# Staging of paired weight blocks: six tiles owned by each phase in place of four shared ones

## The chip, the cores and the metric

The kernel runs on one core of one Trainium2 chip. The metric is the device time of one execution in microseconds; the figure compared is the median of several runs. Profiled executions are taken one at a time, and their views (engine busy shares, waits, chains of waits, timelines) come from a single execution.

## The reference

One decoder layer for 256 tokens of width 4096, all in float32. One projection feeds two mixers: gated linear attention (branch A) and sliding-window attention with sinks (branch B). Each branch is projected to 4096 columns, the two are merged by sigmoid gates, projected once more and added to x.

```
h = rms_norm(x, norm_gains)
z = h @ w_in                       # gq gk gv gg gdec | sq sk sv sg | ga gb
o_a = gla_mix(gq, gk, gv, log_a)   # chunked linear attention, 8 heads
y_a = (rms_norm(o_a) * silu(gg)) @ w_gla_out
o_b = swa_sink_mix(sq, sk, sv, sinks)
y_b = (o_b * silu(sg)) @ w_swa_out
merged = sigmoid(ga + b_gates[0]) * y_a + sigmoid(gb + b_gates[1]) * y_b
out = rms_norm(x + merged @ w_out, final_norm_gain)
```

Nearly all of the work is in products of a 256-row left side with weights that are read once from memory, some 477 MB.

## The kernel before

Every float32 product is made of three matmuls: both operands are split into a high half (a cast on ACT, L141) and a low half (a subtraction on DVE, L142), and hi·hi, hi·lo and lo·hi are summed in PSUM (L160 to L162, L232 to L234). The left sides (hT, oaT, obT, mT) stay in SBUF in both halves; weights stream through.

**Phases.** The program goes through these in order: the blocks gq, gk, gv, gg of branch A (`gemm`, L145); the projection ya of branch A (`spilled`, four pairs of column blocks, ya0 to ya3); branch B (sk, sv, sq, sg with `gemm`, and its attention); the projection yb (yb0 to yb3); eight gate pairs in the order ga0, gb0, ga1, gb1 and so on; 64 transposes that make mT; the last projection o in four pairs; the final norm. The results of ya and yb are spilled to memory and read back by the gates (tiles yga, ygb, fetched by DMAs that ACT issues).

**A pair.** `pair` (L186) multiplies the left side with two column blocks of 512 at once. Its loop runs over blocks j of the depth, 8 in ya and yb, 16 in the gates and o. Each j loads two tiles of 512 KB, r_j and s_j, on SP's queue (L206, L208). For most j there are eight products of a tile and its hi/lo halves: 24 matmuls. For the j in `SEVEN` (0, 2, 5 of 8; 0, 3, 5, 8, 10, 13 of 16) there are seven, 21 matmuls, by a scheme in Strassen's manner: DVE forms sums of the loaded tiles, t in L212 (from r and s), u in L213 and the new s in L214, and four tiles t, u, r, s are split into halves. The left sides of those products are sums too; `combine` (L165) makes them (tiles a and d on DVE, cast and subtraction into xca, xcb, xch or xcm). The first pair of ya, yb and o has eight products at every j, so that its combine can run beside it. For the gates, the combine of hT into xch is run by `then` behind the second pair of yb (L272), and all eight gate pairs have sevens. A pair of 8 with sevens has 183 matmuls, one of 16 has 366, one of 16 without sevens 384. `outputs` (L247) adds the seven sums up; its first sum is held in tile v.

**Buffers.** The loaded tiles (tag raw) come from one pool `stage` with four buffers (L72) that all phases share. Halves come from the pool of the phase `cur["hl"]`, with a ring of three for `gemm` and of five for `pair` (`cur["n"]`); so do t, u and v. The y tiles of the gates and the x tiles of o have a ring of two, tag "yr".

**Order.** The Tile scheduler sets each engine's order; loads, casts and low halves are written at raised priority (PRIO 400 in `gemm`, PRM 120 in `pair`), and each engine runs its list in order. SP issues the weight loads one after the other, and each waits for the last reader of the buffer that it gets.

Of the kernel before, what the change touches and what calls it, by code (L numbers as in the profile page):

```python
# [48 lines left out]
def trunk_kernel(  # L49
# [95 lines left out]
    def gemm(name, lhs, w, nkt, before=None, chunks=WHOLE):  # L145

        acc = [acc_ps.tile([P, NB], F32, tag="acc", name=f"{name}_a{t}") for t in range(NT)]
        for k0, n in [c for c in chunks if c[0] < nkt]:
            if before is not None:
                before(k0, n)  # L150
            with tc.high_priority(PRIO):
                raw = stage.tile([P, n, NB], F32, tag="raw", name=f"{name}_r{k0}")
# [12 lines left out]
    def combine(lhs, xc, js, name):  # L165


        for c, j in enumerate(js):
# [472 lines left out]
    for n in range(NP2):  # L641
# [101 lines left out]
```

## Time and profile before

| | us |
|---|---|
| median of 3 runs (2613.38 to 2619.92) | 2614.85 |
| the profiled execution | 2607.58 |
| its span in the trace | 2605.8 |
| TensorE busy in it | 2503.3 |
| DVE busy in it | 1759.6 |
| ACT busy in it | 1219.4 |

The span runs from the first instruction to the last in the trace. Busy time is the time in which an engine has an instruction running; matmuls are pipelined, so a busy TensorE isn't TensorE at its peak. The phases stand in the trace one behind the other: ya about 600 to 783 us, yb to 1488, the gates to 2215, o to 2591. A "pair" below is the stretch of TensorE's time from its first matmul to the next pair's first.

### The profile page before, as it was taken

The page shows a single profiled execution, that of the slowest core. Times are in us where ns is not written, and L with a number is a line of the kernel's source. Part 1 is how long each engine was busy: PE and PEld are TensorE (multiplying, and loading weights), DVE is VectorE, ACT ScalarE, POOL GpSimd, SP SyncE. Part 2 cuts the span into 40 slices and gives each one's busy share as a digit, 9 for nine tenths or more (in the row PEclk, how much of TensorE's full clock was granted, in tenths as well). Part 3 has the DMA queues.
Part 4 walks back from the last instruction along what each step waited for, and adds up shares of the span by engine and source line. Part 5 has one row for each costly group of instructions (what it writes and reads, how often), then busy time and mean ns, then how long its engine had stood idle before and what let it go on. Part 6 is the DMA issues. An engine that isn't in the chain of part 4 may idle for free.

```text
span 2605.8 us, 29359 instructions
## 1 busy us (share of the span) xinstructions
PE 2503.3 (96%) x10968; PEld 1996.1 (77%) x10968; DVE 1759.6 (68%) x1967; ACT 1219.4 (47%) x1488; POOL 41.9 (2%) x52
## 2 busy tenths in 40 slices
PE   8999999999999999999998999999999999999997
PEld 6778888887777888888786777777787777778765
DVE  7554555546774455555568778878878887857777
ACT  6444354434453344444544444445445445545444
POOL 4000000000000000000000000000000000000000
PEclk9999999999999999999998999999999999999999
DMA  7556556555666645555465666666666666555655
GB/s 254 150 172 187 166 178 185 170 169 166 222 202 202 186 151 175 159 148 184 130 201 163 205 214 203 194 217 198 200 201 207 206 199 220 184 179 193 217 190 190
DMA packets 139024, 491.14 MB, mean 188 GB/s; under 512 B 15840, under 2 KB 16224, under 8 KB 138880
## 3 DMA queue, kind: packets, MB, share of 16 engines
q1 hardware_dynamic: 127296, 461.69, 55.7%
q10 hardware_dynamic: 11584, 27.57, 3.1%
q8 instruction: 86, 1.41, 0.2%
q14 instruction: 58, 0.48, 0.1%
HBM read 476.61 MB, written 12.58 MB: 188 GB/s over the span
## 4 chain that ended last, share of the span: by engine, by line
PE 53%; DVE 24%; DMA 17%; issue 4%; ACT 1%; POOL 0%; ACTq 0%; SPq 0%; DVEq 0%; POOLq 0%
DMA ga_s<-in_wgate_dram 5%; DMA gb_s<-in_wgate_dram 4%; DMA o_s<-in_wout_dram 4%; PE sg_a L161 2%; PE gv_a L161 2%; PE sq_a L162 2%; PE sq_a L160 2%; PE gv_a L160 2%; PE sq_a L161 2%; PE gv_a L162 2%; PE sg_a L160 2%; PE sg_a L162 2%; PE gg_a L162 2%; PE gg_a L160 2%; PE gg_a L161 2%
## 5 line engine op out<-in xcount | busy, mean ns | idle before, releaser
L212 DVE TENSOR_TENSOR gb_t<-gb_r,gb_s 128x1024 f32<-128x1024 f32 x24 | 29.4, 1224 | 28.8 <-DMA gb_s<-in_wgate_dram 28.8
L212 DVE TENSOR_TENSOR ga_t<-ga_r,ga_s 128x1024 f32<-128x1024 f32 x24 | 29.4, 1224 | 24.0 <-DMA ga_s<-in_wgate_dram 24.0
L212 DVE TENSOR_TENSOR o_t<-o_r,o_s 128x1024 f32<-128x1024 f32 x18 | 22.0, 1225 | 32.4 <-DMA o_s<-in_wout_dram 32.3
L101 POOL TENSOR_TENSOR sf<-sf,mhalf 128x1 f32<-128x1 f32 x2 | 1.1, 550 | 1824.5 <-DVE sf L100 1824.5
L119 DVE SCALAR_TENSOR_TENSOR hT<-xsb,gin_sb,hT 128x256 fp32r<-128x256 f32 x32 | 26.1, 865 | 5.3 <-ACT hT L118 5.3
L565 ACT ACTIVATE s<-s,mx 128x128 f32<-128x128 f32 x64 | 28.4, 445 | 0.0
L128 POOL TENSOR_TENSOR ssq<-ssq,sq 128x512 f32<-128x512 f32 x15 | 25.6, 1709 | 24.5 <-ACT sq L127 23.9
L627 ACT ACTIVATE gb_d<-gb_d 128x512 f32<-128x512 f32 x16 | 10.1, 632 | 24.0 <-DVE gb_d L626 23.9
L212 DVE TENSOR_TENSOR ya_t<-ya_r,ya_s 128x1024 f32<-128x1024 f32 x9 | 11.0, 1225 | 14.5 <-DMA ya_s<-in_wgla_dram 14.4
L550 DVE SCALAR_TENSOR_TENSOR s<-s,mask 128x384 f32<-128x384 f32 x32 | 16.0, 552 | 6.0 <-PE s L549 6.0
L212 DVE TENSOR_TENSOR yb_t<-yb_r,yb_s 128x1024 f32<-128x1024 f32 x9 | 11.0, 1223 | 11.5 <-DMA yb_s<-in_wswa_dram 11.5
L656 ACT ACTIVATE xt<-x 128x512 f32<-128x512 f32 x16 | 10.0, 627 | 15.9 <-DVE x L245 15.9
L141 ACT CAST sg_16h<-sg_r 128x1024 fp32r<-128x1024 f32 x4 | 4.2, 1050 | 28.1 <-PE sg_a L162 28.1
L214 DVE TENSOR_TENSOR gb_s<-gb_u,gb_s 128x512 f32<-128x512 f32 x24 | 16.6, 690 | 0.5
L213 DVE TENSOR_TENSOR ga_u<-ga_t,ga_r 128x512 f32<-128x512 f32 x24 | 16.6, 690 | 0.5
L214 DVE TENSOR_TENSOR ga_s<-ga_u,ga_s 128x512 f32<-128x512 f32 x24 | 16.6, 690 | 0.5
L213 DVE TENSOR_TENSOR gb_u<-gb_t,gb_r 128x512 f32<-128x512 f32 x24 | 16.5, 688 | 0.4
L473 DVE COPY oraw<-op 128x512 f32<-128x512 f32 x8 | 5.5, 692 | 15.6 <-PE op L472 15.6
L118 ACT ACTIVATE hT<-xsb,gin_sb 128x256 fp32r<-128x256 f32 x32 | 14.0, 498 | 2.6 <-DMA xsb<-in_xT_dram 2.2
L582 DVE COPY pT<-pt 128x384 f32<-128x384 f32 x16 | 8.9, 555 | 9.3 <-PE pt L579 9.3
L141 ACT CAST gb_t10h<-gb_t 128x1024 fp32r<-128x1024 f32 x4 | 4.2, 1053 | 23.1 <-DVE gb_t L212 17.8
L579 PE MATMUL pt<-ident,s 128*128 128x128 f32 x96 | 15.0, 279 | 0.0
(2815 smaller groups left out, 9027.0 us busy)
## 6 DMA issues: line engine op xcount, KB each, us to landing
gv_r<-in_win_dram SPq DMA_DIRECT2D x64, 512.0 KB, 4.0
gg_r<-in_win_dram SPq DMA_DIRECT2D x64, 512.0 KB, 3.9
sq_r<-in_win_dram SPq DMA_DIRECT2D x64, 512.0 KB, 3.6
sg_r<-in_win_dram SPq DMA_DIRECT2D x64, 512.0 KB, 3.6
ga_r<-in_wgate_dram SPq DMA_DIRECT2D x64, 512.0 KB, 4.8
ga_s<-in_wgate_dram SPq DMA_DIRECT2D x64, 512.0 KB, 5.8
gb_r<-in_wgate_dram SPq DMA_DIRECT2D x64, 512.0 KB, 5.2
gb_s<-in_wgate_dram SPq DMA_DIRECT2D x64, 512.0 KB, 5.6
```

The source lines that it names most:

```text
L118: nc.scalar.activation(hT[:, kt, 0, :], xsb[:, kt, :], AF.Copy, scale=g)
L119: nc.vector.scalar_tensor_tensor(hT[:, kt, 1, :], xsb[:, kt, :], g, hT[:, kt, 0, :].bitcast(F32), ALU.mult, ALU.subtract)
L128: nc.gpsimd.tensor_tensor(ssq, ssq, sq, ALU.add)
L160: nc.tensor.matmul(acc[t], lh, hi[:, i, :], start=kt == 0, stop=False)
L161: nc.tensor.matmul(acc[t], lh, lo[:, i, :], start=False, stop=False)
L162: nc.tensor.matmul(acc[t], ll, hi[:, i, :], start=False, stop=kt == nkt - 1)
L212: nc.vector.tensor_tensor(ts, r1, r2[:, 0:1, :].broadcast_to([P, 2, NB]), ALU.add)
L213: nc.vector.tensor_tensor(t2[:, 0, :], ts[:, 1, :], r1[:, 0, :], ALU.add)
L214: nc.vector.tensor_tensor(r2[:, 0, :], t2[:, 0, :], r2[:, 1, :], ALU.add)
L550: nc.vector.scalar_tensor_tensor(s4[:, jj * 2 + half, :], sps[:, 0 : 3 * P], HD**-0.5, mask2, ALU.mult, ALU.add)
L565: nc.scalar.activation(s4[:, k, cs], s4[:, k, cs], AF.Exp, bias=mx[:, k, t : t + 1], accum_out=sm[:, k, t : t + 1],)
L579: nc.tensor.transpose(tp[:, m * P : (m + 1) * P], s4[:, k, m * P : (m + 1) * P], ident)
```

## The change

The staging tiles `raw` no longer come from a pool that all phases share, but from the pool of the phase, with `cur["r"]` buffers: four where `gemm` runs and six where `pair` runs (ya; yb, gates and o). v of `outputs` moves into the ring "yr" of two, which the gates' y tiles and o's x tiles use; d of `combine` shares the buffer of t; xcb and xch share one buffer, and st and sf one with "ev". Because xch can now be written only when yb is done with xcb, the combine of hT moves from behind yb1 to behind ga0's products, and ga0 has eight products at every j, 384 matmuls in place of 366.

```diff
-    stage = ctx.enter_context(tc.tile_pool(name="stage", bufs=4))
...
-                raw = stage.tile([P, n, NB], F32, tag="raw", name=f"{name}_r{k0}")
+                raw = cur["hl"].tile([P, n, NB], F32, tag="raw", name=f"{name}_r{k0}", bufs=cur["r"])
...
-            d = cur["hl"].tile([P, 4, P], F32, tag="v", name=f"{name}d{j}")
+            d = cur["hl"].tile([P, 4, P], F32, tag="t13", name=f"{name}d{j}")
...
-                r1 = stage.tile([P, 2, NB], F32, tag="raw", name=f"{name}_r{j}")
+                r1 = cur["hl"].tile([P, 2, NB], F32, tag="raw", name=f"{name}_r{j}", bufs=cur["r"])
                 nc.sync.dma_start(r1, w[j][:, 0:2, :])
-                r2 = stage.tile([P, 2, NB], F32, tag="raw", name=f"{name}_s{j}")
+                r2 = cur["hl"].tile([P, 2, NB], F32, tag="raw", name=f"{name}_s{j}", bufs=cur["r"])
...
-    def outputs(q, d, name):
+    def outputs(q, d, name, pool):
 
         if 1 in q:
-            v = cur["hl"].tile([P, NB], F32, tag="v", name=f"{name}_v")
+            v = pool.tile([P, NB], F32, tag="yr", name=f"{name}_v", bufs=2)
...
-            if n == 1 and then is not None:
-                then()
...
     with phase("hl0") as cur["hl"], phase("gla") as gp:
-        cur["n"] = STG
+        cur["n"], cur["r"] = STG, 4
...
     with phase("hl1") as cur["hl"], phase("yap") as yp:
-        cur["n"] = STM
+        cur["n"], cur["r"] = STM, 6
...
     with phase("hl2") as cur["hl"], phase("swa") as sp:
-        cur["n"] = STG
+        cur["n"], cur["r"] = STG, 4
...
-    cur["hl"], cur["n"] = ctx.enter_context(phase("hl3")), STM
-    cur["n"] = STM
+    cur["hl"] = ctx.enter_context(phase("hl3"))
+    cur["n"], cur["r"] = STM, 6
     xp = ctx.enter_context(phase("xp"))
+    ep = ctx.enter_context(phase("ep"))
+    xcb = xp.tile([P, len(SEVEN[OKT // 2]), 4, 2, P], F32R, tag="xc", name="xcb")
+    spilled("yb", obT, wswa, yb_d, xcb, ep)
     xch = xp.tile([P, len(SEVEN[KT // 2]), 4, 2, P], F32R, tag="xc", name="xch")
-    with phase("ybp") as yp:
-        xcb = yp.tile([P, len(SEVEN[OKT // 2]), 4, 2, P], F32R, name="xcb")
-        spilled("yb", obT, wswa, yb_d, xcb, yp, lambda: combine(hT, xch, SEVEN[KT // 2], "h"))
-    ep = ctx.enter_context(phase("ep"))
...
-            q = pair(f"{kind}{n}", hT, wgate[w * NP2 + n], KT // 2, xc=xch)
+            q = pair(f"{kind}{n}", hT, wgate[w * NP2 + n], KT // 2, xc=None if n + w == 0 else xch)
+            if n + w == 0:
+                combine(hT, xch, SEVEN[KT // 2], "h")
...
-    st = ep.tile([P, NT, NBLK], F32, name="st")
+    st = ep.tile([P, NT, NBLK + 1], F32, tag="ev", name="st")
```

The order of SP's loads is the same in both kernels. What moves stands on DVE and ACT, at three places. Rows are one engine's list, each line an instruction with the tile that it writes and those that it reads; line numbers of the changed kernel are lower by one to three.

DVE at the passage from yb1 to yb2, before, in two pieces: the first sums of yb2, then the combine of hT (ha, hd, xch), which begins here,

```order
L212 TENSOR_TENSOR yb2_t0_10023<-yb2_r0_10019,yb2_s0_10021 128x1024
L245 TENSOR_TENSOR yb_d1_9944<-yb1_q5_9619,yb_d1_9944 128x512
L175 TENSOR_TENSOR hd0_9959<-ha0_9957 128x128
L176 TENSOR_TENSOR hd0_9959<-ha0_9957 128x128
L177 TENSOR_TENSOR hd0_9959<-hd0_9959,ha0_9957 128x128
L142 TENSOR_TENSOR yb2_t0l_10029<-yb2_t0_10023,yb2_t0h_10028 128x1024
L178 TENSOR_TENSOR hd0_9959<-ha0_9957,hd0_9959 128x128
L170 TENSOR_TENSOR ha3_9966<-hT_87 128x512
L180 TENSOR_TENSOR xch_9287<-hd0_9959,xch_9287 128x4x128
```

and some thirty rows further its end, with what follows of yb2:

```order
L178 TENSOR_TENSOR hd13_10004<-ha13_10002,hd13_10004 128x128
L213 TENSOR_TENSOR yb2_u0_10024<-yb2_t0_10023,yb2_r0_10019 128x512
L180 TENSOR_TENSOR xch_9287<-hd13_10004,xch_9287 128x4x128
L214 TENSOR_TENSOR yb2_s0_10021<-yb2_u0_10024,yb2_s0_10021 128x512
L142 TENSOR_TENSOR yb2_u0l_10033<-yb2_u0_10024,yb2_u0h_10032 128x512
L142 TENSOR_TENSOR yb2_r0l_10037<-yb2_r0_10019,yb2_r0h_10036 128x1024
L142 TENSOR_TENSOR yb2_s0l_10041<-yb2_s0_10021,yb2_s0h_10040 128x1024
```

The same place now:

```order
L211 TENSOR_TENSOR yb2_t0_9965<-yb2_r0_9961,yb2_s0_9963 128x1024
L141 TENSOR_TENSOR yb1_s7l_9913<-yb1_s7_9906,yb1_s7h_9912 128x1024
L212 TENSOR_TENSOR yb2_u0_9966<-yb2_t0_9965,yb2_r0_9961 128x512
L141 TENSOR_TENSOR yb2_t0l_9971<-yb2_t0_9965,yb2_t0h_9970 128x1024
L213 TENSOR_TENSOR yb2_s0_9963<-yb2_u0_9966,yb2_s0_9963 128x512
L141 TENSOR_TENSOR yb2_u0l_9975<-yb2_u0_9966,yb2_u0h_9974 128x512
L244 TENSOR_TENSOR yb1_v_9941<-yb1_q6_9616,yb_d1_9940 128x512
L211 TENSOR_TENSOR yb2_t2_10047<-yb2_r2_10043,yb2_s2_10045 128x1024
L141 TENSOR_TENSOR yb2_r0l_9979<-yb2_r0_9961,yb2_r0h_9978 128x1024
```

All rows of ha, hd and xch are gone from between yb2's t0 and u0; they stand from behind yb3's fifth block into ga0.

ACT at the start of ya (oaT is its left side, made from transposes oa3_t0 and oa3_t2), before:

```order
L278 CAST oaT_803<-oa3_t0_4224 128x2x256
L141 CAST ya0_r0h_4255<-ya0_r0_4251 128x1024
L141 CAST ya0_s0h_4259<-ya0_s0_4253 128x1024
L141 CAST ya0_r1h_4291<-ya0_r1_4287 128x1024
L141 CAST ya0_s1h_4295<-ya0_s1_4289 128x1024
L278 CAST oaT_803<-oa3_t2_4231 128x2x256
```

and now:

```order
L275 CAST oaT_800<-oa3_t0_4221 128x2x256
L275 CAST oaT_800<-oa3_t2_4228 128x2x256
L613 DMA bt00_10633<-in_bgates_dram 128x1024
L178 CAST xca_4243<-yad0_4545 128x4x128
L140 CAST ya0_r0h_4252<-ya0_r0_4248 128x1024
L140 CAST ya0_s0h_4256<-ya0_s0_4250 128x1024
```

The second cast of oaT, a load of the gates' bias and the first cast of xca have moved ahead of the first half ya0_r0h.

DVE in ga2, where the gate of gb1 is finished, from the use of its second y tile (ygb101) to that of its fourth, before:

```order
L245 TENSOR_TENSOR gb_d1_13375<-gb_d1_13375,ygb101_13392 128x512
L626 SCALAR_TENSOR_TENSOR gb_d1_13375<-gb_d1_13375,rstd_81,bt11_12729 128x512
L245 TENSOR_TENSOR m_10693<-m_10693,gb_d1_13375 128x512
L142 TENSOR_TENSOR ga2_r4l_13589<-ga2_r4_13584,ga2_r4h_13588 128x1024
L142 TENSOR_TENSOR ga2_s4l_13593<-ga2_s4_13586,ga2_s4h_13592 128x1024
L245 TENSOR_TENSOR gb_d1_13375<-gb_d1_13375,ygb110_13398 128x512
L626 SCALAR_TENSOR_TENSOR gb_d1_13375<-gb_d1_13375,rstd_81,bt11_12729 128x512
L245 TENSOR_TENSOR m_10693<-m_10693,gb_d1_13375 128x512
L212 TENSOR_TENSOR ga2_t5_13624<-ga2_r5_13620,ga2_s5_13622 128x1024
L245 TENSOR_TENSOR gb_d1_13375<-gb_d1_13375,ygb111_13404 128x512
```

and now:

```order
L244 TENSOR_TENSOR gb_d1_13298<-gb_d1_13298,ygb101_13315 128x512
L624 SCALAR_TENSOR_TENSOR gb_d1_13298<-gb_d1_13298,rstd_78,bt11_12652 128x512
L244 TENSOR_TENSOR m_10632<-m_10632,gb_d1_13298 128x512
L141 TENSOR_TENSOR ga2_r4l_13512<-ga2_r4_13507,ga2_r4h_13511 128x1024
L624 SCALAR_TENSOR_TENSOR gb_d1_13298<-gb_d1_13298,rstd_78,bt11_12652 128x512
L141 TENSOR_TENSOR ga2_s4l_13516<-ga2_s4_13509,ga2_s4h_13515 128x1024
L244 TENSOR_TENSOR gb_d1_13298<-gb_d1_13298,ygb110_13321 128x512
L211 TENSOR_TENSOR ga2_t5_13547<-ga2_r5_13543,ga2_s5_13545 128x1024
L244 TENSOR_TENSOR m_10632<-m_10632,gb_d1_13298 128x512
L244 TENSOR_TENSOR gb_d1_13298<-gb_d1_13298,ygb111_13327 128x512
```

Between the two uses stand eight rows in both lists; what is new is that the buffer of ygb111 is that of ygb101, and that one step of the gate and the addition to m have changed places with s4l and t5.

## Rows read from the trace of the kernel before

**Rows 1.** The page, part 1: busy time, share of the span and instructions

```profile
PE 2503.3 (96%) x10968; PEld 1996.1 (77%) x10968; DVE 1759.6 (68%) x1967; ACT 1219.4 (47%) x1488; POOL 41.9 (2%) x52
```

**Rows 2.** Stretches: length, busy time of each engine, granted clock, DMA share, GB/s

```profile
649.10:691.50 42.40, 42.40 (x185) 34.44 (x184) 33.53 (x35) 22.13 (x25) 0.00 (x0) 1.00 0.64 211
691.50:783.00 91.50, 87.06 (x368) 70.05 (x367) 68.79 (x75) 42.63 (x45) 1.34 (x4) 0.98 0.62 207
1341.40:1383.80 42.40, 42.40 (x184) 34.45 (x183) 33.08 (x38) 20.15 (x23) 0.00 (x0) 1.00 0.67 211
1383.80:1442.00 58.20, 45.26 (x185) 35.36 (x183) 47.29 (x70) 24.43 (x29) 0.00 (x0) 0.88 0.49 163
1442.00:1488.30 46.30, 43.25 (x185) 34.08 (x184) 36.63 (x40) 22.17 (x25) 0.00 (x0) 1.00 0.62 205
1488.30:1577.30 89.00, 86.29 (x367) 68.36 (x366) 67.31 (x70) 41.30 (x46) 0.00 (x0) 1.00 0.65 213
1577.30:2215.20 637.90, 612.27 (x2579) 483.10 (x2577) 518.82 (x564) 315.49 (x348) 0.00 (x0) 0.99 0.62 204
2316.00:2591.40 275.40, 261.56 (x1099) 205.76 (x1097) 212.63 (x232) 132.34 (x162) 0.55 (x1) 0.99 0.59 192
```

**Rows 3.** Waits of TensorE: total, times, longest

```profile
PE yb_q L232 <- ACT yb_u0h L141: 12.7, 1, 12.7
PE ga_q L233 <- DVE ga_t5l L142: 6.4, 4, 1.8
...
PE sk_a L161 <- DVE sk_0l L142: 1.4, 1, 1.4
```

**Rows 4.** Waits of all engines, same columns: DVE's for loads

```profile
DVE o_t L212 <- DMA o_s<-in_wout_dram: 32.3, 15, 3.9
DVE gb_t L212 <- DMA gb_s<-in_wgate_dram: 28.8, 20, 2.7
...
DVE ga_t L212 <- DMA ga_s<-in_wgate_dram: 24.0, 17, 3.9
```

**Rows 5.** Chain of waits, 1696 to 1716: start, us, what

```profile
1698.61 0.60 DVE ga_u L213
...
1704.43 1.14 DVE ga_r6l L142
1705.56 1.15 DVE ga_s6l L142
...
1706.73 6.90 DMA ga_s<-in_wgate_dram
...
1713.65 1.24 DVE ga_t L212
```

**Rows 6.** The page, part 6: DMA issues, KB each, us to landing

```profile
ga_s<-in_wgate_dram SPq DMA_DIRECT2D x64, 512.0 KB, 5.8
...
sk_r<-in_win_dram SPq DMA_DIRECT2D x16, 512.0 KB, 4.4
...
ygb<-yb_d ACTq DMA_DIRECT2D x16, 256.0 KB, 4.4
```

**Rows 7.** Timeline of DVE, yb1 to yb2: start, us, what

```profile
1380.09 0.28 DVE L175 TENSOR_TENSOR hd<-ha 128x128 f32<-128x128 f32 x1
1380.29 0.29 DVE L176 TENSOR_TENSOR hd<-ha 128x128 f32<-128x128 f32 x1
...
1396.55 0.69 DVE L213 TENSOR_TENSOR yb_u<-yb_t,yb_r 128x512 f32<-128x512 f32 x1
```

**Rows 8.** Timeline at the start of ya, same columns

```profile
600.63 0.58 ACT L278 CAST oaT<-oa_t 128x512 fp32r<-128x512 f32 x1 [2.17 <-PE oa_t L288]
601.11 1.05 ACT L141 CAST ya_r0h<-ya_r 128x1024 fp32r<-128x1024 f32 x1
601.25 0.69 DVE L279 TENSOR_TENSOR oaT<-oa_t,oaT 128x512 fp32r<-128x512 f32 x1 [0.52 <-ACT oaT L278]
...
602.21 2.07 PE L232 MATMUL ya_q<-ya_r0h,oaT 128*128 128x512 f32 x4 [0.98 <-ACT ya_r0h L141]
```

More of the change, by code (lines that the diff above doesn't have):

```diff
@@ L260, in outputs, with spilled @@
                 nc.scalar.copy(d[t][i], q[b])
-    def spilled(name, lhs, w, dst, xc, pool, then=None):
+    def spilled(name, lhs, w, dst, xc, pool):
         for n in range(NP2):
@@ L266, in spilled @@
             d = pool.tile([P, NT, 2, NB], F32, tag="ev", name=f"{name}_d{n}")
-            outputs(q, [[d[:, t, i, :] for i in range(2)] for t in range(NT)], f"{name}{n}")
+            outputs(q, [[d[:, t, i, :] for i in range(2)] for t in range(NT)], f"{name}{n}", pool)
             for t in range(NT):
@@ L310, in trunk_kernel @@
         rms_scale(rstd, xps[:, 0:NT], DM)
-        wd_raw = stage.tile([P, KT, RANK], F32, tag="raw", name="wd_raw")
+        wd_raw = cur["hl"].tile([P, KT, RANK], F32, tag="raw", name="wd_raw", bufs=cur["r"])
         nc.sync.dma_start(wd_raw, wdec)
@@ L617, in trunk_kernel @@
             nc.scalar.dma_start(bt, bgates[w, 2 * n * NB : 2 * (n + 1) * NB].partition_broadcast(P).rearrange("p (i c) -> p i c", i=2))
-            q = pair(f"{kind}{n}", hT, wgate[w * NP2 + n], KT // 2, xc=xch)
+            q = pair(f"{kind}{n}", hT, wgate[w * NP2 + n], KT // 2, xc=None if n + w == 0 else xch)
+            if n + w == 0:
+                combine(hT, xch, SEVEN[KT // 2], "h")
             d = ep.tile([P, NT, 2, NB], F32, tag="ev", name=f"{kind}_d{n}")
-            outputs(q, [[d[:, t, i, :] for i in range(2)] for t in range(NT)], f"{kind}{n}")
+            outputs(q, [[d[:, t, i, :] for i in range(2)] for t in range(NT)], f"{kind}{n}", ep)
             for t in range(NT):
@@ L646, in trunk_kernel @@
         cs = [slice((2 * n + i) * NB, (2 * n + i + 1) * NB) for i in range(2)]
-        outputs(q, [[x2[:, t, cs[i]] for i in range(2)] for t in range(NT)], f"o{n}")
+        outputs(q, [[x2[:, t, cs[i]] for i in range(2)] for t in range(NT)], f"o{n}", ep)
         gf = ep.tile([P, 2, NB], F32, tag="bt", name=f"gf{n}")
@@ L658, in trunk_kernel @@
     for t in range(NT):
-        sf = ep.tile([P, 1], F32, name=f"sf{t}")
-        nc.vector.tensor_reduce(sf, st[:, t, :], AX.X, ALU.add)
+        sf = st[:, t, NBLK:]
+        nc.vector.tensor_reduce(sf, st[:, t, :NBLK], AX.X, ALU.add)
         rms_scale(sf, sf, DM)
```

## The prediction

> **What bounds the kernel now.** I read the page's busy shares first, since the engine that is nearly full sets what can be won. TensorE is busy in 2503.3 of 2605.8 us, DVE in 68% [rows 1]. So the kernel stands on its matmuls, and what a change without less arithmetic can win is TensorE's stalls. They are not spread evenly. The stretches by pair of blocks [rows 2] show that (line by line: ya1; ya2 and ya3; yb1; yb2; yb3; ga0; gb0 to gb3; o1 to o3): the second pair of the first output projection (ya1) takes 42.40 us with TensorE busy for all of them, and yb1 the same. Those pairs have 183 matmuls, so 42.40 / 183 = 0.2317 us is what one costs in a stream without a stall, and a pair of 366 (gates, last projection) has a floor of 84.80 us, one of 384 a floor of 88.97. The other pairs stand above it. ya2 and ya3 together are 91.50 - 84.80 = 6.7 above, yb2 58.20 - 42.40 = 15.8, yb3 3.9, the seven gate pairs from gb0 to gb3 637.90 - 7 x 84.80 = 44.3, o1 to o3 275.40 - 254.40 = 21.0. That is 91.7 us, in thirteen pairs of one kind and in yb2. Part of it is the clock: behind the long wait in yb2 the granted clock of the stretch is 0.88, so some of it ran at 1.2 GHz in place of 2.4; what the waits lose, the clock gives back with them, and I count both together.
>
> Next, who is late. TensorE's own waits name ga_t5l and its like, low halves that DVE writes [rows 3]; DVE in turn waits 32.3, 28.8 and 24.0 us for the loads of o, gb and ga [rows 4], always in L212, the first sum of a seven-product block, which needs both tiles r and s of its block. The chain of waits in one gate pair shows why [rows 5]: the load of ga_s goes out at 1706.73, right behind the end of the last low half that used its slot, takes 6.90 us, and L212 starts at 1713.65. The loads have four slots, two blocks, so a block's load goes out when the block two before it is done with, and DVE has only the block between to work on meanwhile. The median load of ga_s takes 5.8 us to land [rows 6]; an eight-product block between gives DVE two low halves at 1.14 us each, 2.3. The DMA engines as such have room: their share in the gate stretch is 0.62 [rows 2].
>
> **Part 1, six slots in the pairs.** A block's load now goes out when the block three before it is done, so one more block lies in between. The sevens sit at blocks 0, 3, 5, 8, 10 and 13. For block 5, DVE now has blocks 3 and 4 to do while the load travels. By the pieces of the chain a 1024-wide step costs DVE 1.14 and a 512-wide one 0.60, so a seven is 1.14 + 0.60 + 0.60 for the sums and 3 x 1.14 + 0.60 for the low halves, 6.36; an eight is 2.28. That is 8.6 us of work against 5.8 of travel, where it was 2.3. For blocks 3 and 8 there are two eights, 4.6 against 5.8: 1.2 can stay in the worst case, less what DVE is ahead.
>
> Is DVE then itself too slow? At the head of a pair it also carries the pair before: eight adds of the outputs (8 x 0.60 = 4.8) and the gate's elementwise work (12 steps, 7.2). With blocks 0 to 5 (three sevens 19.1, three eights 6.8) that makes 37.9 us. TensorE needs (3 x 21 + 3 x 24) x 0.2317 = 31.3 for these blocks. But DVE may run ahead by the hi/lo rings, which hold five: four tiles of the eights at the end of the pair before, at 12 matmuls each, are 4 x 12 x 0.2317 = 11.1 us. 31.3 + 11.1 = 42.4, so 37.9 fits with 4.5 to spare. I walked DVE's new order through blocks 0 to 5 by these costs: every low half is ready before its matmul, the tightest (t5l) by 0.8 us. A margin that thin won't hold in every pair, so I don't take zero: I leave 1.33 us per gate pair, 2.0 per o pair (two loads of x share the new ring there) and 1.8 for each of ya2, ya3, yb2, yb3.
>
> Gates: 44.3 - 7 x 1.33 = 35.0 won. ya2, ya3, yb2, yb3: 6.7 + 15.8 + 3.9 - 4 x 1.8 = 19.2. o1 to o3: 21.0 - 3 x 2.0 = 15.0. Sum 69.2.
>
> Of the 19.2, yb2's share has another cause, and goes for another reason. There TensorE waits 12.7 us for yb_u0h [rows 3], because DVE works through the sums for the gates' left side (combine of hT) from 1380.09 and gets to yb_u only at 1396.55 [rows 7]. In the changed order nothing stands between yb2_t0l and yb2_s0; the combine comes behind yb3_r5l and reaches into the first gate pair, which no longer needs its result. What hides it there: that pair has only eights, 16 x 2.28 = 36.5 us of DVE, with the outputs of yb3 41.3; the combine takes at most the 16.5 us from 1380.09 to 1396.55 [rows 7]. That is 57.8 of DVE's time in some 89 of TensorE's.
>
> A rule speaks against part 1. In the gate stretch DVE is busy for 518.82 of 637.90 us (81%) and weight loads for 483.10 (76%) [rows 2]. The Trainium skill (Perfetto Trace Analysis, Identifying the Most-Contended Engine) judges a vector engine by its occupancy and TensorE by its weight-load share rather than by its matmul share, and says of the fullest engine "Optimize this engine first". By it DVE would bound the gates, and deeper staging would give nothing there. ya1 and yb1 speak against it, where TensorE is full with DVE at 33 of 42; DVE's waits for loads [rows 4] too.
>
> **Part 2, eight products in ga0.** 18 more matmuls: 18 x 0.2317 = 4.2. The pair took 89.00 with 366; with 384 the floor is 88.97, without the sevens' stalls, and I leave 0.7. So +0.7.
>
> **Part 3, staging that belongs to a phase.** The shared slots let the loads of the next phase go out while the last pair still ran. Now the first tiles of a phase lie over tiles of the one before and wait for their last reader. Three places: the starts of ya, swa and yb. At ya's start ACT before made one cast for oaT at 600.63, the first half ya_r0h at 601.11, and the first product began at 602.21 [rows 8]. The new order puts two casts of oaT and one of xca ahead of ya0_r0h, and the latter waits for DVE's low half of oaT, the second one, and four sums of 0.2 [rows 7]: 601.25 + 2 x 0.69 + 0.8 brings xca's cast to about 603.4, it takes some 0.6 as the one for oaT, so ya0_r0h starts near 604.0 and the first product 1.1 later as it does now, near 605.1: +3.0 with rounding. The same at yb. At swa, sk_0h lies over ya3_s7l, whose last reader is the last matmul of ya; the cast (1.0) now follows it, and the loads of sk_r2 and sk_r4 wait for ya3_s7h, 4.4 us of travel [rows 6] against the 12 matmuls of the first tile (2.8): 1.0 + 1.7 = +2.7 beside the wait of 1.4 that stands there today [rows 3]. Together +8.7. No row shows such a start, so bounds: 0 if the order hides it, and three whole landings of about 4.7 us, 14, if each waits for one.
>
> **Part 4, the ring shared by v and the loads of y and x.** Before, the gates' y tiles were fetched a pair ahead; now v and y take turns in two buffers. The third and fourth y go out when the first two are used. By the new order eight steps of DVE lie between the use of ygb101 and that of ygb111, three 1024-wide and five 512-wide, 6.4 us, against 4.4 to land [rows 6]. I cost it at nothing; the cover is those steps. If it were gone, 4.4 each. On ACT the issue of ygb101 now waits for v's last reader with the cast ga2_s0h queued behind it; that reader stands two steps of 0.60 behind v itself, and TensorE has the three tiles t0, u0 and r0 ahead of s0, so nothing for it either, and 1.2 a pair if they ran out.
>
> **Sum.** -69.2 + 0.7 + 8.7 = -59.8. Profiled execution: 2607.58 - 59.8 = 2547.8. It lies 7.3 below the median of the runs, 2614.85; the same gain from there gives 2555.
>
> **The rivals.** *Half.* The rings of five, not the loads, hold DVE back as soon as the loads are early; its low halves then wait for TensorE to free a tile, and the 4.5 us to spare are not there. Half of 69.2 is 34.6; with +9.4 that is -25: 2590. For it: margins under 1 us; against it: the walk. *DVE is the bound:* 37.9 us of work against 31.3, no lead, 6.6 lost per pair as today (44.3 / 7 = 6.3). Only yb2's combine is won: -14.0 + 9.4 = -4.6: 2610. Against it: 37.9 counts only a head of a pair, and DVE sits idle for 19% of the stretch. (It is what the Trainium skill's rule above would have.) *Slower:* the y loads. If DVE reaches the third and the fourth y less than 4.4 us after it used the first and second, it stands in front of both, with all low halves of the blocks behind them queued. Eight gate pairs x 2 x 4.4 = 70; half of it is covered by the lead. 35 + 9.4 - 14.0 = +30: 2645. It decides at 4.4 us between two uses; the order gives 6.4. *Better:* no stalls remain in the pairs (-22.5) and the starts cost half (-4.4): 2528.
>
> **How the numbers follow.** Forecast 0.68 (2555), half 0.17 (2590), DVE the bound 0.05 (2610), slower 0.05 (2645), better 0.05. The range: downward, half of the 22.5 us of stalls left in the pairs gone (-11.2) and 3 us less at the starts give 2541; upward it reaches to the half case, 2590, which also covers starts at 14. Outside are the other three cases and the far side of two, under 2 in 10. A change under 0.3% (7.8 us) is one that measurement can't tell from none. Faster: forecast, half and better, 0.90. Same: DVE the bound, 0.05. Slower: 0.05.
>
> **What would show it.** Right, if ga1 to gb3 take 85 to 87 us each, DVE's waits in L212 for the gates fall from some 53 us to under 15, and yb2 stands near 44. The starts: the first product of ya about 4 us behind the last transposes. Wrong, if L212's waits are gone and the pairs still take 90 (then it's DVE or the rings: look at what its low halves wait for), or if DVE waits for yga and ygb by name, or if a start takes over 8 us.

## The result and the profile after

The changed kernel takes 2537.69 us (median of 3 runs, 2536.68 to 2538.5) against 2614.85 before: a ratio of 0.970 with an interval of 0.9678 to 0.9722, 77 us less. The direction and the place were forecast, the size was not: 2555 was the forecast and 2541 the low end of its range.

The page of the changed kernel, part 1, in the form of [rows 1]: TensorE is busy for 22 us less, though it has 18 matmuls more, and its span is 2536.8.

```profile
PE 2481.7 (98%) x10986; PEld 1999.1 (79%) x10986; DVE 1726.4 (68%) x1929; ACT 1222.5 (48%) x1479; POOL 42.2 (2%) x52
```

The stretches in the form of [rows 2]: ya2 and ya3; yb2 and yb3; ga0; gb0 to gb3; o1 to o3.

```profile
694.50:784.60 90.10, 86.26 (x367) 67.97 (x365) 69.45 (x77) 39.61 (x42) 0.00 (x0) 1.00 0.56 181
1390.60:1480.60 90.00, 86.24 (x367) 68.07 (x366) 76.31 (x91) 45.04 (x49) 0.00 (x0) 1.00 0.70 228
1480.60:1569.90 89.30, 89.28 (x384) 72.43 (x385) 51.58 (x63) 36.50 (x39) 0.00 (x0) 1.00 0.62 193
1569.90:2165.40 595.50, 595.50 (x2580) 483.98 (x2578) 512.37 (x556) 319.14 (x348) 0.00 (x0) 1.00 0.68 219
2267.70:2522.70 255.00, 254.68 (x1099) 206.41 (x1097) 212.93 (x233) 136.08 (x162) 0.55 (x1) 1.00 0.64 204
```

The seven gate pairs take 595.50 us and TensorE is busy for all of them. Six of them take 84.80 us each, the floor itself; the last, gb3, takes 86.6, because its stretch ends with 16 transposes of m that make the first tiles of mT (timeline of TensorE; they stand in the stretch of the kernel before too):

```profile
2163.54 1.91 PE L285 MATMUL m_t<-ident,m 128*128 128x128 f32 x16
```

So no stall is left in the gates. o1 to o3 stand at 255.0, three floors of 84.8 are 254.4. The granted clock there is 1.00 where it was 0.99. What is left above the floor, but for 0.6 us in o2, is in the four pairs of ya and yb: 90.1 and 90.0 against 84.8, some 2.6 a pair.

The page, part 5, DVE's first sums that stood in [rows 4] (busy, mean ns, idle time ahead and what ended it):

```profile
L211 DVE TENSOR_TENSOR gb_t<-gb_r,gb_s 128x1024 f32<-128x1024 f32 x24 | 29.3, 1220 | 8.9 <-DMA gb_s<-in_wgate_dram 8.9
...
L211 DVE TENSOR_TENSOR o_t<-o_r,o_s 128x1024 f32<-128x1024 f32 x18 | 22.0, 1222 | 11.6 <-DMA o_s<-in_wout_dram 11.6
...
L211 DVE TENSOR_TENSOR ga_t<-ga_r,ga_s 128x1024 f32<-128x1024 f32 x18 | 22.0, 1221 | 5.5 <-DMA ga_s<-in_wgate_dram 5.4
```

DVE waits for loads of the gates for 14.3 us in place of 52.8. The start of ya, as in [rows 8]:

```profile
603.95 0.62 ACT L178 CAST xca<-yad 128x512 fp32r<-128x512 f32 x1 [1.79 <-DVE yad L177]
...
604.47 1.04 ACT L140 CAST ya_r0h<-ya_r 128x1024 fp32r<-128x1024 f32 x1
...
605.56 1.65 PE L231 MATMUL ya_q<-ya_r0h,oaT 128*128 128x512 f32 x3 [4.19 <-ACT ya_r0h L140]
```

and TensorE's waits at the three starts (ya, yb, and sk for branch B; of the lines shown in [rows 3] only the one at sk is of a start):

```profile
PE yb_q L231 <- ACT yb_r0h L140: 4.2, 1, 4.2
PE ya_q L231 <- ACT ya_r0h L140: 4.2, 1, 4.2
...
PE sk_a L159 <- ACT sk_0h L140: 2.3, 1, 2.3
```

The term of the starts is thus right to a microsecond: the forecast had ya0_r0h at 604.0 and the first product at 605.1, the trace 604.47 and 605.56. Its path at ya is right too: what holds the first product is ACT's cast ya_r0h, which stands behind the cast of xca, and that one waits for DVE.

By segments of the two profiled executions the account is this. The starts are what the first products of ya and yb come later (602.21 to 605.56 at ya; at yb a wait of 4.2 where it was 1.3), and what branch B between them is longer by besides:

| term | forecast, us | measured, us |
|---|---|---|
| gate pairs gb0 to gb3 | -35.0 | 637.9 to 595.5: -42.4 |
| ya2, ya3, yb2, yb3 | -19.2 | 91.5 + 104.5 to 90.1 + 90.0: -15.9 |
| o1 to o3 | -15.0 | 275.4 to 255.0: -20.4 |
| ga0 | +0.7 | 89.0 to 89.3: +0.3 |
| starts of ya, yb, swa | +8.7 | 3.4 + 2.9 + 3.3 = +9.6 |
| o0, ya0, yb0 and the rest | 0 | -0.2 |
| sum of the spans | -59.8 | 2605.8 to 2536.8: -69.0 |
| from medians | -59.8 | 2614.85 to 2537.69: -77.2 |

So there are two gaps to explain: 9 us between the sum and the spans, and 8 us between the spans and the medians.

### The profile page after: what moved, and what is told of

Read it like the earlier page. It is cut to its first block, busy times and chain, and to the rows that moved or that the text cites. A ratio compares the mean times of both kernels' runs of the same rounds, so it can differ in the third digit from the quotient of the medians.

```text
span 2536.8 us, 29365 instructions
## 1 busy us (share of the span) xinstructions
PE 2481.7 (98%) x10986; PEld 1999.1 (79%) x10986; DVE 1726.4 (68%) x1929; ACT 1222.5 (48%) x1479; POOL 42.2 (2%) x52
## 4 chain that ended last, share of the span: by engine, by line
PE 90%; DVE 4%; DMA 2%; issue 1%; ACT 1%; POOL 0%; SPq 0%; ACTq 0%; POOLq 0%; DVEq 0%
PE ga_q L233 5%; PE ga_q L231 5%; PE ga_q L232 5%; PE gb_q L233 4%; PE gb_q L232 4%; PE gb_q L231 4%; PE o_q L232 4%; PE o_q L233 4%; PE o_q L231 4%; PE sg_a L160 2%; PE gv_a L160 2%; PE sq_a L160 2%; PE gv_a L159 2%; PE sq_a L159 2%; PE gv_a L161 2%; PE sq_a L161 2%
## 5 line engine op out<-in xcount | busy, mean ns | idle before, releaser
L211 DVE TENSOR_TENSOR gb_t<-gb_r,gb_s 128x1024 f32<-128x1024 f32 x24 | 29.3, 1220 | 8.9 <-DMA gb_s<-in_wgate_dram 8.9
L211 DVE TENSOR_TENSOR o_t<-o_r,o_s 128x1024 f32<-128x1024 f32 x18 | 22.0, 1222 | 11.6 <-DMA o_s<-in_wout_dram 11.6
L211 DVE TENSOR_TENSOR ga_t<-ga_r,ga_s 128x1024 f32<-128x1024 f32 x18 | 22.0, 1221 | 5.5 <-DMA ga_s<-in_wgate_dram 5.4
L211 DVE TENSOR_TENSOR ya_t<-ya_r,ya_s 128x1024 f32<-128x1024 f32 x9 | 11.0, 1222 | 9.6 <-DMA ya_s<-in_wgla_dram 9.6
L654 ACT ACTIVATE xt<-x 128x512 f32<-128x512 f32 x16 | 10.1, 629 | 13.2 <-DVE x L244 13.2
L211 DVE TENSOR_TENSOR yb_t<-yb_r,yb_s 128x1024 f32<-128x1024 f32 x9 | 11.0, 1221 | 7.8 <-DMA yb_s<-in_wswa_dram 7.8
L461 POOL TENSOR_SCALAR_AFFINE_SELECT ats<-ats 128x128 f32<-128x128 f32 x16 | 8.0, 523 | 423.7 <-DVE ats L459 423.7
L473 ACT ACTIVATE jk<-oraw 128x256 f32<-128x256 f32 x16 | 6.7, 417 | 16.9 <-DVE oraw L470 16.6
L285 PE MATMUL m_t<-ident,m 128*128 128x128 f32 x64 | 10.2, 301 | 4.5 <-DVE mT L276 4.5
L576 PEld LDWEIGHTS pt<-ident,s 128*128 128x128 f32 x96 | 11.2, 145 | 4.3 <-ACT s L562 3.7
```

Of the source, the lines that this page charges most:

```text
L211: nc.vector.tensor_tensor(ts, r1, r2[:, 0:1, :].broadcast_to([P, 2, NB]), ALU.add)
L576: nc.tensor.transpose(tp[:, m * P : (m + 1) * P], s4[:, k, m * P : (m + 1) * P], ident)
```

## The experiments

The kernels were measured in four sets, each beside the kernel before: its median was 2614.9 beside the changed kernel, 2614.1 beside s4_own, s4_shared and s6_shared4, and 2611.3 beside the others (single executions 2606 to 2626). Between kernels of two sets a difference of some 4 us in the medians therefore says little by itself; where one is used below, the stretches of the traces stand beside it.

| kernel | median, us | lowest to highest | runs |
|---|---|---|---|
| changed kernel (own tiles, 6) | 2537.7 | 2536.7 to 2538.5 | 3 |
| own tiles, 4 (s4_own) | 2618.2 | 2609.2 to 2624.4 | 10 |
| shared tiles, 4 (s4_shared) | 2605.0 | 2599.4 to 2612.2 | 10 |
| own tiles, 5 (s5_own) | 2532.9 | 2532.1 to 2534.4 | 4 |
| 4 shared, 6 in pairs (s6_shared4) | 2526.8 | 2524.9 to 2529.3 | 4 |
| 4 shared, 5 in pairs (s5_shared4) | 2520.4 | 2519.1 to 2522.4 | 4 |
| 4 shared, 5 in ya and yb, 6 in gates and o (s5_s6_shared4) | 2522.6 | 2520.6 to 2523.9 | 4 |
| halves' ring of 4 (ring4) | 2563.4 | 2561.3 to 2566.5 | 4 |
| 4 more sums in block 5 (dve_plus4) | 2573.0 | 2570.3 to 2575.1 | 4 |
| 1 more sum in block 5 (dve_plus1) | 2539.2 | | 1 |

**Is it the staging, or the order that came with it?** Two kernels keep everything else of the change and go back to four tiles, one with tiles of the phase, one with the shared pool.

```diff
-        cur["n"], cur["r"] = STM, 6
+        cur["n"], cur["r"] = STM, 4
```

> The changed kernel with four staging tiles per phase in place of six, nothing else different. Theory (the fifth and sixth tile bring the gain in the pairs): DVE's waits in L211 for the loads of the gates and o come back to 70 to 90 us, the seven gate pairs from gb0 to gb3 take about 638 us again in place of 595.5, o1 to o3 about 275 in place of 255.0, so 2537.7 + 42 + 20 + some 3 = 2600. Rival (the new order of DVE, sums of the next pair ahead of the outputs, or the combine that moved brings it): the gate pairs stay near 85 each and the time near 2540.

The stretches gb0 to gb3 and o1 to o3 of s4_own, and DVE's waits for the gates' loads in it (total, times, longest):

```profile
1580.40:2228.70 648.30, 615.33 (x2579) 480.85 (x2577) 513.96 (x557) 313.26 (x348) 0.00 (x0) 0.99 0.62 200
2330.30:2601.40 271.10, 259.32 (x1099) 204.62 (x1097) 212.01 (x231) 131.09 (x161) 0.00 (x0) 1.00 0.61 194
```

```profile
DVE gb_t L211 <- DMA gb_s<-in_wgate_dram: 35.6, 21, 4.2
...
DVE ga_t L211 <- DMA ga_s<-in_wgate_dram: 21.2, 12, 3.2
```

The stalls are back, 648.3 and 271.1 us; 2618.2 is a ratio of 1.0021 (1.0009 to 1.0034) to the kernel before. It is 18 us more than the 2600 expected, 10 of them in the gates (648.3 for 638). What the change brings besides the two tiles wins nothing in the gates and o together.

For the second, the tiles are taken in turn, the first four from a pool that lives through the whole program, as before:

```diff
+    stage = ctx.enter_context(tc.tile_pool(name="stage", bufs=4))
...
+    def rawt(shape, name):
+        i = cur["i"] % cur["r"]
+        cur["i"] += 1
+        if i < 4:
+            return stage.tile(shape, F32, tag="raw", name=name)
+        return cur["hl"].tile(shape, F32, tag="raw", name=name, bufs=cur["r"] - 4)
```

> The changed kernel with the four staging tiles of one shared pool as in the kernel before; ga0 with eight products, the moved combine and the ring shared by v and y stay. Theory: only the move of the combine is won (yb2 near 44.5 in place of 58.2) and the starts of ya, swa and yb are as before, so 2614.9 - 14 = 2600; against four tiles per phase it is faster by what the starts cost, 8 to 10 us. Rival (order, not staging): about 2530.

Its stretches of yb2, gb0 to gb3 and o1 to o3:

```profile
1383.20:1429.80 46.60, 44.40 (x185) 35.53 (x184) 36.56 (x40) 21.80 (x23) 0.00 (x0) 0.96 0.63 203
1570.20:2213.20 643.00, 612.31 (x2580) 479.30 (x2578) 512.74 (x556) 312.53 (x348) 0.00 (x0) 1.00 0.62 202
2313.60:2583.50 269.90, 259.12 (x1099) 205.08 (x1097) 212.04 (x231) 131.46 (x161) 0.00 (x0) 1.00 0.60 195
```

yb2 is at 46.6 in place of 58.2 though the loads have four slots: that part is the combine's, as forecast. The time, 2605.0 where 2600 was expected, is 9 below the kernel before (0.9974, 0.9960 to 0.9988); the 12 won in yb2 are partly lost where the gates take 643.0, 5 more than in [rows 2]. Between four and six tiles lie 80.5 us with own tiles (2618.2 to 2537.7) and 78.2 with shared ones (2605.0 to 2526.8).

One thing these runs don't separate. The scheduler makes a new order for each number of tiles. TensorE's order in the gate pair ga2 is the same with four, five and six tiles but for one row of 366; on DVE some 19 of 82 rows stand elsewhere with four tiles than with six. So shown is what the two tiles bring together with the order that the scheduler makes for them; six tiles in the order of four were not run.

**How many tiles does it take?**

> The changed kernel with five staging tiles per phase in the pairs in place of six. Theory (cover of the load by DVE's work): with five, the slot of s5 is that of r3, so DVE has s3l, r4l and s4l, 3.4 us, to do while the load of s5 travels for about 5; 1.5 us short, and ga_t5l is ready only 0.4 us ahead of its use in the changed kernel. So stalls of about 1 us per gate and o pair, against 6 with four tiles: 2537.7 + 10 = 2548 (2542 to 2560). Rival (the sixth tile does nothing, five are enough): 2538. Rival (only whole blocks count, two tiles each): near the 2618 of four.

The stretches ya2, gb0 to gb3 and o1 to o3 of s5_own, DVE's waits for the gates' loads, and TensorE's wait for t5l:

```profile
695.00:737.40 42.40, 42.40 (x185) 34.45 (x184) 36.25 (x40) 21.82 (x23) 0.00 (x0) 1.00 0.69 223
1562.40:2162.30 599.90, 596.92 (x2580) 483.55 (x2578) 511.69 (x556) 317.29 (x348) 0.00 (x0) 1.00 0.66 217
2263.80:2518.60 254.80, 254.79 (x1099) 206.35 (x1097) 213.05 (x233) 135.05 (x162) 0.55 (x1) 1.00 0.63 207
```

```profile
DVE gb_t L211 <- DMA gb_s<-in_wgate_dram: 27.6, 21, 2.7
...
DVE ga_t L211 <- DMA ga_s<-in_wgate_dram: 14.5, 12, 2.5
```

```profile
PE ga_q L232 <- DVE ga_t5l L141: 2.7, 3, 1.7
```

Five tiles are not worse than six, which no theory had (2548 was expected): the median is 5 us lower, the span of the profiled execution 4.2 (2532.6 for 2536.8). As ratios to the kernel before, 0.9696 and 0.970, the two aren't told apart. My working for block 5 was right in kind: TensorE does wait for ga_t5l, 2.7 us in three pairs, and the gates stand at 599.9, 4.4 above the changed kernel. What I missed is ya2, at 42.40, its floor. And DVE's waits for loads, 42 us in the gates, are not far from those of [rows 4] (53) with almost no loss: the waits as such don't price anything. With four tiles (s4_own) 57 us of them go with gates that are 52.8 longer than in the changed kernel, with five 42 us with gates that are 4.4 longer.

**Why do ya2 to yb3 lose with six?** In their order of the changed kernel, TensorE's products of block 2 (t2) stand ahead of block 0's last ones (q4, q2), and DVE's sum and low half of t2 ahead of the drain of the pair before. TensorE's wait in ya2 of the changed kernel:

```profile
PE ya_q L231 <- DVE ya_d L244: 1.8, 1, 1.8
```

It waits for ya_d, the drain. DVE has nothing to do just before, since the sum t2 stands ahead of the drain in its list and waits for its load:

```profile
691.75 1.23 DVE L211 TENSOR_TENSOR ya_t<-ya_r,ya_s 128x1024 f32<-128x1024 f32 x1 [2.47 <-DMA ya_s<-in_wgla_dram]
```

With five tiles the scheduler doesn't pull block 2 forward: in ya2 of s5_own the first product of t2 comes at 705.4, behind all of blocks 0 and 1. The next kernel takes five in ya and yb and six after, four of them shared.

> Five staging tiles in ya and yb and six in the gates and o, four of them from one pool shared by all phases. Theory: with six, the order of TensorE in ya2, ya3, yb2 and yb3 has the products of block 2 ahead of block 0's q4 and q2 and of the drain of the pair before, which costs some 2.5 us per pair; with five it has not. So ya2 to yb3 at 42.4 each, the gates at 84.8, the starts as with the shared pool: 2526.8 - 10 = 2517. Rival (the pairs with six are late for another reason, such as the combine of ya and yb): 2527.

Its stretches of ya2, ga0 and gb0 to gb3:

```profile
691.50:733.90 42.40, 42.40 (x185) 34.45 (x184) 36.16 (x40) 21.80 (x23) 0.00 (x0) 1.00 0.67 223
1466.40:1557.60 91.20, 91.20 (x385) 73.28 (x386) 51.56 (x63) 35.76 (x38) 0.00 (x0) 0.98 0.60 184
1557.60:2153.10 595.50, 595.50 (x2580) 483.99 (x2578) 512.53 (x556) 318.77 (x348) 0.00 (x0) 1.00 0.68 219
```

ya2 is at the floor and the gates too, so the pairs lose by the six tiles and the order that comes with them, and not by the combine; that it is the order is read from the rows above, since number and order changed together. The median is 2522.6 where 2517 was expected, because the passage from five to six costs something of its own: ga0 takes 91.2 at a clock of 0.98 in place of 89.3, and yb3 is longer by 3.4 at its end. The gain of six over five in the gates is smaller than that.

> Five staging tiles in all pairs, four of them shared. Theory: the ya and yb pairs at their floor, the ga pairs lose some 1 us each at t5l as with five tiles per phase (0.6, 1.9 and 0.9 there): 2517 + 4 = 2521; the shared pool is worth 10 to 12 against five of the phase's own, 2532.9. Rival (in the gates five are as good as six): 2517.

Its stretches of ya2, gb0 to gb3 and o1 to o3:

```profile
690.60:733.00 42.40, 42.40 (x184) 34.45 (x183) 36.28 (x40) 21.92 (x23) 0.00 (x0) 1.00 0.69 225
1551.50:2150.50 599.00, 596.35 (x2579) 483.76 (x2577) 512.12 (x556) 317.43 (x348) 0.00 (x0) 1.00 0.66 217
2251.00:2505.40 254.40, 254.40 (x1099) 206.47 (x1097) 212.90 (x233) 135.10 (x162) 0.55 (x1) 1.00 0.63 207
```

2520.4 was measured, 2521 expected. This is the lowest median of all, 2 us under the kernel with five and six, whose runs overlap with its own. It is 0.9651 (0.9636 to 0.9665) of the kernel before, the changed kernel 0.970 (0.9678 to 0.9722): 17 us less by the medians, some 13 by the ratios.

**What do tiles of the phase's own cost?**

> The changed kernel with six staging tiles in the pairs, of which four are of a pool shared by all phases and two are the phase's own. Theory: the gate and o pairs stay at their floor, and the starts of ya, swa and yb (first product 3.4 us later in the changed kernel at ya, a wait of 4.2 at yb, some 3 at sk) go back to those of the kernel before: 2537.7 - 9 = 2529. Rival (the starts are late because of the new order alone, not because of the overlaid tiles): 2537.

Its stretches of ya, ya2 and gb0 to gb3:

```profile
602.40:780.10 177.70, 173.63 (x742) 139.20 (x743) 134.21 (x150) 87.44 (x95) 0.00 (x0) 1.00 0.62 204
689.90:734.90 45.00, 43.06 (x185) 34.11 (x184) 36.05 (x39) 21.71 (x23) 0.00 (x0) 1.00 0.66 211
1560.20:2155.70 595.50, 595.50 (x2580) 484.59 (x2578) 512.09 (x556) 318.94 (x348) 0.00 (x0) 1.00 0.68 219
```

The first product of ya is at 602.40 in place of 605.56 and ya2 keeps its 45.0. 2526.8 is 10.9 under the changed kernel; with five tiles the same step is worth 12.4 (2532.9 to 2520.4), with four 13.2. The forecast's 8.7 for the three starts was of the right size. With the shared pool ACT's list at ya has ya_r0h right behind the first cast of oaT again (at 601.30). In the changed kernel the first load of ya was under way from 581.56 to 587.17, long before; what tiles of the phase's own cost at ya is thus an order on ACT and not a late load, as the forecast had it.

**How thin is the margin?** In the changed kernel ga_t5l ends at 1849.57 + 1.22 = 1850.79 and the product that reads it starts at 1851.20, in ga2 (timeline of DVE, then of TensorE):

```profile
1849.57 1.22 DVE L141 TENSOR_TENSOR ga_t5l<-ga_t,ga_t5h 128x1024 fp32r<-128x1024 f32 x1
```

```profile
1851.20 0.39 PE L232 MATMUL ga_q<-ga_t5l,xch 128*128 128x512 f32 x1
```

That is 0.4 us, less than the 0.8 of my walk, and it is the same in ga1, ga2 and ga3. To see what it bears, L211 of block 5 is done more than once:

```diff
-                    nc.vector.tensor_tensor(ts, r1, r2[:, 0:1, :].broadcast_to([P, 2, NB]), ALU.add)
+                    for _ in range(1 + (4 if j == 5 and npr == 16 else 0)):
+                        nc.vector.tensor_tensor(ts, r1, r2[:, 0:1, :].broadcast_to([P, 2, NB]), ALU.add)
```

> The same with L211 of block 5 done twice: 1.15 us more per pair. Theory: the three ga pairs lose 0.75 each, gb and o pairs nothing, since their margins at t5l, r5l and s5l are over 1.8: 2537.7 + 2 = 2540, and the profile shows stalls at block 5 of ga1, ga2, ga3 alone. Rival (margins as thin as 0.4 us are used up by jitter, so any more work costs in full): ten pairs lose 1.15: 2549.

Its stretches of ga1, gb1 and gb0 to gb3:

```profile
1656.50:1741.50 85.00, 85.00 (x367) 68.73 (x367) 75.97 (x84) 44.94 (x49) 0.00 (x0) 1.00 0.67 216
1741.50:1826.30 84.80, 84.80 (x367) 68.91 (x367) 73.86 (x80) 45.26 (x49) 0.00 (x0) 1.00 0.69 217
1571.70:2167.80 596.10, 596.10 (x2580) 483.40 (x2578) 520.71 (x563) 318.39 (x348) 0.00 (x0) 1.00 0.69 218
```

Less than even the small loss that I expected: 0.2 in ga1, nothing in gb1. The orders tell why. In the kernel before, the product of ga_t5h is followed at once by that of ga_t5l, for which TensorE waits. In the changed kernel both products of ga_t5h (for q5 and q7) stand ahead of that of ga_t5l, 0.23 us more for DVE; in dve_plus1 those of ga_u5h, ga_r5h and ga_s5h are pulled ahead of the low halves' as well. The scheduler made another order for the longer DVE work, with high products first, and a small lag is hidden by it. So this run, a single one, shows that the work costs nothing clear of noise; it doesn't show what the order of the changed kernel would bear.

> The changed kernel in which L211 of block 5 is done five times in place of once in the ten pairs of 16 blocks with sevens: 4.6 us more of DVE work per pair, directly ahead of t5l, where the least is to spare (0.4 us in the ga pairs of the changed kernel, 2.5 to 3 in gb at r5l and r6l, about 2 in o). Theory (the margin at that place alone decides): ga pairs lose 4.2, gb and o pairs about 2, in all 3 x 4.2 + 4 x 2 + 3 x 2.2 = 27: 2565. Rival (DVE's idle time in the pair, some 12 us, takes it up): 2538. Rival (delays add up from pair to pair): 10 x 4.6 = 46 and more, 2584.

The stretches of gb0, ga1, gb1 and o1 to o3 of dve_plus4:

```profile
1575.20:1660.10 84.90, 84.90 (x368) 68.95 (x368) 75.12 (x80) 45.40 (x51) 0.00 (x0) 1.00 0.68 216
1660.10:1750.50 90.40, 86.84 (x367) 69.55 (x366) 79.79 (x87) 44.96 (x49) 0.00 (x0) 0.98 0.64 203
1750.50:1837.50 87.00, 85.48 (x367) 68.77 (x366) 77.20 (x83) 44.80 (x49) 0.00 (x0) 1.00 0.66 211
2295.70:2558.50 262.80, 259.23 (x1099) 208.42 (x1097) 227.72 (x245) 134.94 (x162) 0.55 (x1) 0.99 0.61 198
```

ga1 loses 5.6, gb1 2.2, o1 to o3 7.8 in all, gb0 nothing. The losses don't add up from pair to pair: ga1, ga2 and ga3 take 90.5 each, gb1 and gb2 87.0. TensorE now waits for the cast of t5 itself (10.9 us in the three ga pairs). In ga1 it waits 3.5 us, a little less than the 4.2 expected; the other 2 us are longer busy time for the same products (86.84 for 84.80) at a mean granted clock of 0.98: behind the wait a part of the stretch ran at 1.2 GHz in place of 2.4, and I had not costed that. The sum is 35 us in the median, 31 of it in the gates and o, where I had 27, and neither 0 (idle time of DVE takes it up) nor 46 and more (delays add up).

**What does the ring of halves do?**

```diff
-STM = 5
+STM = 4
```

> The changed kernel with rings of four for the high and low halves in the pairs in place of five. Theory of the prediction (the ring's lead lets DVE carry the outputs and gates at a pair's head): the lead falls by one tile, 12 matmuls of 0.2317, 2.8 us, and since ga_t5l has only 0.4 us to spare, three ga pairs lose 2.4 each, gb and o pairs 1 to 2.5 each, in all some 20: 2558. Rival (the loads were all; DVE has time enough, 14% idle): 2538.

The stretches of ya2, yb2, gb0 to gb3 and o1 to o3 of ring4, and TensorE's longest waits in ya and yb:

```profile
694.90:744.00 49.10, 44.61 (x185) 35.41 (x184) 36.68 (x41) 21.89 (x23) 0.00 (x0) 0.97 0.59 193
1402.00:1450.40 48.40, 44.56 (x185) 35.42 (x185) 36.88 (x41) 21.91 (x23) 0.00 (x0) 0.96 0.60 196
1588.20:2185.50 597.30, 596.95 (x2580) 483.11 (x2578) 513.69 (x556) 319.95 (x348) 0.00 (x0) 1.00 0.66 218
2289.10:2550.60 261.50, 257.86 (x1099) 206.96 (x1097) 214.94 (x234) 137.32 (x163) 0.55 (x1) 0.99 0.62 201
```

```profile
PE ya_q L231 <- DVE ya_d L244: 8.8, 4, 3.6
PE yb_q L231 <- DVE yb_d L244: 7.4, 3, 3.6
```

The time came out as expected, 2563 for 2558, at another place. The gates lose 1.8 us in all; by the forecast's own sum a ring of four gives 31.3 + 3 x 2.78 = 39.6 for 37.9 us of work, which still fits. The loss is in ya and yb, where ya2 and yb2 take 4 more than with a ring of five (49.1 and 48.4) and TensorE waits for the drain ya_d and yb_d, and in o1 to o3 (261.5 for 255.0). My expectation was thus right by accident: the ring's fifth tile does not carry the gates.

**Why do medians and spans differ?**

> The kernel before, unchanged, profiled again. Question: its profiled execution was 2607.6 and its three timed runs 2613 to 2620, so the gain counted in spans (69) and in medians (77) differ by 8. Theory: the stalls for loads vary from one execution to the next, so a second profile shows other gate and o pairs above the floor, with a sum of 6 to 12 us more; the pairs without a stall (ya1, yb1) stay at 42.4. Rival: the difference lies outside the span, and the pairs take the same times again.

The profiled execution of that run took 7840 us, and no row of it is used; its nine others took 2606 to 2620. A second profile:

> The kernel before, unchanged, for a second undisturbed profile. The one on record took 2607.6, the median of 25 runs is 2614.1. Theory: its stalls for loads are not the same in each execution; the pairs that differ from the first profile are gate and o pairs, by 0.5 to 3 us each, with ya1 and yb1 at 42.4 in both; a run near 2614 has some 6 us more there. Rival: pairs the same, the difference lies elsewhere.

This execution took 2617.9 us. Its stretches of ya1; ya2 and ya3; yb2; gb0 to gb3; o1 to o3, as in [rows 2]:

```profile
648.80:691.20 42.40, 42.40 (x185) 34.49 (x184) 32.48 (x34) 22.03 (x25) 0.00 (x0) 1.00 0.65 211
691.20:787.20 96.00, 88.60 (x368) 71.32 (x367) 70.16 (x77) 43.01 (x46) 1.97 (x4) 0.96 0.60 197
1387.70:1448.20 60.50, 45.53 (x185) 35.29 (x184) 48.23 (x71) 25.05 (x30) 0.00 (x0) 0.89 0.47 156
1583.60:2223.50 639.90, 611.69 (x2580) 480.67 (x2578) 516.04 (x560) 313.48 (x347) 0.00 (x0) 1.00 0.62 203
2325.60:2602.50 276.90, 264.32 (x1099) 208.54 (x1097) 213.63 (x233) 133.37 (x162) 0.55 (x1) 0.98 0.59 192
```

ya1 is at 42.40 in both. ya2 and ya3 take 4.5 more than in the first profile, yb2 2.3 more, the gates 2.0, the o pairs 1.5: together 10.3, as much as the two executions differ by (the other segments cancel out). Two thirds of it are in ya2, ya3 and yb2 rather than in the gates and o where I had expected it, with a granted clock of 0.96 for 0.98 in ya2 and ya3. So the stalls differ from one execution to the next, and the profile that I worked from had few of them.

## Why the prediction was off

**Bounds and mechanism: right.** TensorE's stalls in thirteen pairs and yb2 were what could be won, they hung on loads that went out too late, and a longer staging, with the order that the scheduler makes for it, removes them: with four tiles they are back in either form of the pool. Most of yb2's share was the combine's (58.2 to 46.6 with four tiles). The starts cost 9.6 for 8.7, ga0 0.3 for 0.7, the ring of v and y nothing, as costed.

**The step that failed** is in part 1: "A margin that thin won't hold in every pair, so I don't take zero", with 1.33 us left per gate pair and 2.0 per o pair. It holds in every gate pair. The least margin is 0.4 us, half of what the walk gave, and it is the same in ga1, ga2 and ga3, so the gates stand at their floor; dve_plus4 shows that losses don't add up from pair to pair. A margin over zero counted as zero stall there; what I left was a guess without a row behind it, 15.3 us for gates and o, of which 0.6 in o were stalls. Another 1.9 in the gates (595.5 - 593.6) were the transposes in gb3, which my floor of seven times 84.80 had left out. In ya2, ya3, yb2 and yb3 I left 7.2 and 10.5 stayed, from an order that I had seen in the list and not costed: block 2's products ahead of the drain. The low end of the range, 2541, kept half of that residue, and the whole of the offset that follows.

**The second step** is "the same gain from there gives 2555". The gain was summed on a profile 7.3 us under the median. Had that offset been a constant outside the pairs, it would have stayed. It was made, as far as one more profile shows (before_look), of stalls that vary, and these went with the rest: the changed kernel's profiled execution, 2538.5, lies within 1 us of its median, and its 3 runs spread by 1.8 us where 25 of before spread by 12 (2606.1 to 2618.4) and ten of either kernel with four tiles by 13 to 15. With a floor reached, the sum should have ended at the profile's own 2547.8, without the offset: less the 12.8 us of residue that weren't there, with ya and yb's 3.3 more and the starts' 0.9, it is 2539.2, against 2538.5.

**The rivals.** *Half* failed: the rings of five don't hold DVE back, nor do rings of four in the gates. *DVE is the bound* failed: TensorE is busy for 595.5 of 595.5 us with DVE at 512.4 (86%). By the Trainium skill's rule (Perfetto Trace Analysis, Identifying the Most-Contended Engine), as far as it goes by weight loads (484.0 us, 81%) and not by MFU, which was not worked out, DVE would be the engine to work on there. Here DVE is idle for 14% of the stretch, and 1.15 us more of its work per pair lengthened the seven gate pairs by 0.6 us in all (dve_plus1, 596.1 for 595.5, one run), so the measurement decides against the rule. *Slower* by the y loads failed: DVE has no wait for yga or ygb in the trace; for the x loads, which share that ring in o, it has two, 2.6 us in all. *Better* was right in that the gates kept no stall and o only 0.6 us, and wrong in that the starts would cost half.

## What to carry to other kernels

Where a kernel repeats one order from pair to pair, work out for one pair whether each operand is ready before its use. If it is, cost the stall near zero even where the margin is thin (0.4 us was enough here). If not, cost the shortage once per pair, and the time at the lower clock behind it (here 2 us on top of a wait of 3.5). Take the sum to the floor of the engine that then runs without a gap, with everything that runs in the stretch in the floor. Be wary of a single profile of a kernel that waits for loads: its stalls vary from one execution to the next, and here they went together. A pool that belongs to a phase costs something at each of the phase's borders, at ya through the order on ACT; four shared tiles and one of the phase's own gave here what six own ones did and 13 to 17 us more.

## What was not expected of the hardware

The loads of the gates, each some 4.4 to 5 us under way, leave no trace in TensorE's time with six tiles: the three ga pairs have the same 0.4 us of margin to a tenth. And DVE's waits for loads say little by themselves: with four tiles 56.8 us of them stand in gates that are 648.3 - 595.5 = 52.8 above those without a stall, with five 42.1 us in gates that are 4.4 above them.
